# One decoder layer of 512 tokens in f32 on one core: the order of each engine's instructions, up to the second pair of gate's tiles, written in the kernel as lists

## The chip, the cores and the metric

The kernel runs on one core of a Trainium2 chip. The core has five engines with a queue of instructions each: PE (TensorE, matmuls, with a second row PEld for loading weights into the array), DVE (VectorE), ACT (ScalarE), POOL (GpSimd) and SP (SyncE, which here only issues transfers). ACT and POOL issue transfers too. An engine runs its own instructions in the order in which they stand in its queue; between engines, semaphores hold an instruction back until its inputs are made and its output's place is free.

The metric is the device time of one execution in microseconds (us), the median of several runs.

## The reference

One layer of a hybrid decoder: 512 tokens, width 2048, all in float32. The input projection feeds eight forgetting-attention heads (FoX) and eight heads of a sparse attention (NSA) with a compressed, a selected and a windowed branch; their outputs go through one output projection, and a SwiGLU feed-forward of width 5632 follows.

```python
h = _rms_norm(x, attn_norm)
proj = h @ w_in                       # FoX q, k, v, forget gate; NSA q, three k/v pairs, gates
...
s = einsum("bqhd,bkhd->bhqk", qf_b, kf) * scale + cq[..., None] - cum_f[:, :, None, :]
o_fox = einsum("bhqk,bkhd->bqhd", softmax(s, causal), vf)
...
o_nsa = g[0] * o_c + g[1] * o_s + g[2] * o_w
x = x + concat([o_fox, o_nsa]) @ w_out
h = _rms_norm(x, ffn_norm)
x = x + (silu(h @ w_gate) * (h @ w_up)) @ w_down
```

## The kernel before

**Arithmetic.** Every operand of a matmul is held as two parts of the type fp32r, a high part and a low part. ACT makes the high part by a copy that rounds (`split`, lines 87 and 192), DVE then subtracts it from the value to make the low part (lines 84 and 193), and PE adds up three products: high by high, high by low, low by high (`mm` and `mm3t`, line 254). So each operand costs one step on ACT, one on DVE behind it, and PE can't finish with it before both. Large projections are done in a form with seven products of half-size blocks in the place of eight; the sums of blocks that this needs ("forms", made by DVE at lines 991 to 1009 from the input, by `sums` for the weights of gate and up) are operands as well.

**Stages.** In order of time: the first projection with warm-up matmuls ahead of it (0 to 50 us); the projections of NSA's keys and values and their norms (to about 200 us); the heads of NSA and the first of FoX, interleaved with the projections that feed the next ones (to 440 us); the other FoX heads, with projections in the seven-product form (to 640 us); the output projection, `po` (to 795 us); gate and up, `q`, in 22 pairs of column tiles with four weight tiles each (to 1626 us); the down projection, `pd`, to the end.

In attention, a head's scores `s_f` (or `s_s`, `s_w`) go from PE to DVE, which adds the bias `nbf` that POOL made and takes maxima and sums into the statistics `st_f` (line 617); ACT applies the exponential (line 623) and scales (line 632); PE turns the result (`pT_f`, line 648), ACT and DVE split the turned copy into `pt_f`, and PE multiplies it by the values. For the norms of q and k, squares `sq` and `sb` are added, split into `fr_...` (the high part by ACT, the low one by DVE) and summed over the head by a matmul with ones (`ss_...`, line 483).

**What sets the order.** The kernel emits its instructions from Python generators that are advanced by hand, piece by piece. The framework has a planner that then arranges the instructions of each engine by costs and priorities of its own, keeping the dependencies. Two things fix the order in parts: `add_manual_dep` with the class PACE, which ties a transfer behind an instruction of another engine, and `tc.keep_in_program_order`, which is applied through `pin` to whatever `tt` (DVE) and `act` (ACT) emit once `pinned[0]` is set: to "compute" in the output projection (line 1543) and to "all" behind it (line 1580), where `load` (transfers issued by SP) is kept in order as well. Ahead of line 1543 all of the order is the planner's.

**Gate's start.** `fetch` loads a weight tile into a buffer (`r`, `ca` or `cb`), `sums` makes its sums on DVE (three steps of line 84), and `parts` makes the high part on ACT and the low part on DVE. Tile 0 is in `r`, tile 1 in `cb`. A tile then serves 2 x 14 products of its high part and 14 of its low part. Between these stand the last forms of the layer's input: `raw6` and `raw7`, whose parts go into `bigm`, and the residual `x1_15`.

The loop over gate and up:

```python
for j in range(NJ):
    for which in range(2):
        ...
        for g in range(NG):
            i = (2 * j + which) * NG + g
            if 3 <= i < LAST - 1:
                sums(i + 2)
            if 3 <= i < LAST:
                parts(i + 1)
                fetch(i + 4)
            ...
            w = split_w.pop(i)
```

Of the kernel before, what the change touches and what calls it, by code (L numbers as in the profile page):

```python
# [12 lines left out]
OP = mybir.AluOpType  # L13
# [60 lines left out]

@with_exitstack
def hybrid_layer(ctx: ExitStack, tc: tile.TileContext, xT, vec, ffb, wfg, wfirst, win, cmpw, wout, wos, wgu, wdn, out):
    nc = tc.nc
    pinned = [False]

    def pin(ins):  # L80
        return tc.keep_in_program_order(ins) if pinned[0] else ins

    def tt(*args, op):
        return pin(nc.vector.tensor_tensor(*args, op=op))  # L84

    def act(*args, **kw):
        return pin(nc.scalar.activation(*args, **kw))  # L87
# [40 lines left out]
    def sum_weights(after, steps=None):  # L128

        step = next(wsums if steps is None else steps, None)  # L130
        if step is not None:
            d = nc.gpsimd.dma_start(step[0], step[1], **step[2])  # L132
            tc.add_manual_dep(d.ins, after.ins.name, PACE)
# [51 lines left out]
    def split(dst, src, scale=None, neg=None):  # L185

        if scale is None:
            h = act(dst[:, 0], src, AF.Copy)
            tt(dst[:, 1], src, dst[:, 0].bitcast(F32), op=OP.subtract)
            return h  # L190
        else:
            nc.scalar.activation(dst[:, 0], src, AF.Copy, scale=scale)
            nc.vector.scalar_tensor_tensor(dst[:, 1], src, scale, dst[:, 0].bitcast(F32),
                                           op0=OP.mult, op1=OP.subtract)
# [4 lines left out]
    def split2(dst, src, scale=None):  # L199
# [4 lines left out]
        else:  # L204
            h = act(dst[0], src, AF.Copy, scale=scale)
            nc.vector.scalar_tensor_tensor(dst[1], src, scale, dst[0].bitcast(F32), op0=OP.mult, op1=OP.subtract)
# [46 lines left out]
    def mm(o, w, x, j=1, **kw):  # L253
        nc.tensor.matmul(_like(o, j), w, _in_turn(x, j), **kw)  # L254
# [6 lines left out]
    def mm3(o, lh, ll, rh, rl, start, stop):  # L261
        nc.tensor.matmul(o, lh, rh, start=start, stop=False)
        nc.tensor.matmul(o, lh, rl, start=False, stop=False)  # L263
        nc.tensor.matmul(o, ll, rh, start=False, stop=stop)
# [46 lines left out]
    nc.scalar.dma_start(vt, vec)  # L311
# [7 lines left out]
    nc.vector.memset(onesf, 1.0)  # L319
    ones = pers.tile([P, P], FR, name="ones")  # L320
    nc.vector.tensor_copy(ones, onesf)

    def rsqrt(dst, src, n, tmp, whole=True):

        nc.scalar.activation(dst, src, AF.Ln, scale=1.0 / n, bias=EPS)
        nc.scalar.activation(dst, dst, AF.Exp, scale=-0.5)
        nc.scalar.activation(tmp, dst, AF.Square)
        nc.vector.scalar_tensor_tensor(tmp, src, n * EPS, tmp, op0=OP.add, op1=OP.mult)  # L328
        if whole:
            nc.vector.tensor_scalar(tmp, tmp, -0.5 / n, 1.5, op0=OP.mult, op1=OP.add)  # L330
            nc.vector.tensor_tensor(dst, dst, tmp, op=OP.mult)
        else:
            nc.vector.scalar_tensor_tensor(dst, tmp, -3.0 * n, dst, op0=OP.add, op1=OP.mult)

    def colsum(o, src, fr):

        split2(fr, src)
        nc.tensor.matmul(o, ones, fr[0], start=True, stop=False)
        nc.tensor.matmul(o, ones, fr[1], start=False, stop=True)
# [16 lines left out]
    nc.gpsimd.iota(E, pattern=[[-1, T]], base=384, channel_multiplier=1, allow_small_or_imprecise_dtypes=True)  # L356
    nc.gpsimd.affine_select(E, E, pattern=[[-1, T]], compare_op=OP.is_ge, fill=FAR, base=384, channel_multiplier=1)

    dc = xn.tile([P, NB, 32], F32, name="dc")
    nc.gpsimd.iota(dc, pattern=[[P, NB], [-16, 32]], base=-31, channel_multiplier=1, allow_small_or_imprecise_dtypes=True)  # L360
    mc = xn.tile([P, NB, 32], F32, name="mc")
    nc.vector.tensor_scalar(mc, dc, 0.0, None, op0=OP.is_ge)
    nc.gpsimd.affine_select(dc, dc, pattern=[[P, NB], [-16, 32]], compare_op=OP.is_ge, fill=FAR, base=-31, channel_multiplier=1)

    trif = ftile("trif")
    nc.gpsimd.memset(trif, 1.0)
    nc.gpsimd.affine_select(trif, trif, pattern=[[1, T]], compare_op=OP.is_ge, fill=0.0, base=0, channel_multiplier=-1)

    gains = ap_.tile([P, 6], F32, name="gains")
    nc.vector.tensor_scalar_mul(gains, vt[:, 0:6], -0.5 / HD)  # L370
    nc.vector.tensor_scalar_mul(gains[:, V_NQ:V_NQ + 1], gains[:, V_NQ:V_NQ + 1], -SCALE)
    nc.vector.tensor_scalar_mul(gains[:, V_FQ:V_FQ + 1], vt[:, V_FQ:V_FQ + 1], -SCALE)
# [6 lines left out]
    nc.vector.tensor_tensor(rowsf, ident[:, :64], ident[:, 64:], op=OP.add)  # L379
    rows = xn.tile([P, 64], FR, name="rows")  # L380
    nc.vector.tensor_tensor(rows, rowsf, rowsf[:, 31:32].to_broadcast([P, 64]), op=OP.add)

    rows3 = xn.tile([P, 2, 3, 32], FR, name="rows3")
    for n in range(3):
        nc.vector.tensor_copy(rows3[:, :, n], rows.bitcast(F32).rearrange("p (g c) -> p g c", g=2))
# [7 lines left out]
    def scaled(z, name, early=False):  # L393
        t = oxp.tile([P, T], F32, tag="ox", name=f"t_{name}", bufs=OXB) if early else ftile(f"t_{name}")
        if early:
# [3 lines left out]
            nc.vector.tensor_tensor(t.rearrange("p (l b n) -> p b n l", l=16, b=2), b, c, op=OP.mult)  # L399
        else:  # L400
            nc.vector.tensor_tensor(_apart(t), _mixed(z), _apart(rstd), op=OP.mult)
# [17 lines left out]
    def squares(name, z, laid=_apart):  # L419
# [3 lines left out]
        nc.scalar.activation(_apart(sq[half]), laid(z[half]), AF.Square)  # L423
        nc.scalar.activation(_apart(sb[half]), laid(z[second_half]), AF.Square)
        nc.vector.tensor_tensor(sq[half], sq[half], sb[half], op=OP.add)
        return sq

    def square_sums(name, sq, tag, bufs=1):
# [6 lines left out]
        for i in range(NB):  # L435
            nc.tensor.matmul(o[:, i], fr[:, i * P:(i + 1) * P], ones[:, :2], start=(i == 0), stop=(i == NB - 1), skip_group_check=True)
        return o

    def factors(name, o):
# [4 lines left out]
        nc.vector.tensor_tensor(v, o[:, :, 0], eps_col, op=OP.add)  # L444
        nc.scalar.activation(y, v, AF.Ln, scale=1.0 / n)
        nc.scalar.activation(y, y, AF.Exp, scale=-0.5)
        nc.scalar.activation(w, y, AF.Square)
        nc.vector.tensor_tensor(w, v, w, op=OP.mult)
        nc.vector.tensor_scalar(w, w, -0.5 / n, 1.5, op0=OP.mult, op1=OP.add)
        nc.vector.tensor_tensor(qs, w, y, op=OP.mult)  # L450
        nc.vector.scalar_tensor_tensor(iqs, v, 1.0 / n, qs, op0=OP.mult, op1=OP.mult)
# [18 lines left out]
    def normed(name, gain, tag, bufs=5):  # L470
# [5 lines left out]
        nc.scalar.activation(sq[half], t[half], AF.Square)  # L476
        nc.vector.tensor_tensor(sb[half], t[second_half], t[second_half], op=OP.mult)
        nc.vector.tensor_tensor(sq[half], sq[half], sb[half], op=OP.add)
# [4 lines left out]
        nc.tensor.matmul(o, ones, fr, start=True, stop=True)  # L483
# [3 lines left out]
        nc.vector.scalar_tensor_tensor(t, t, gain, y, op0=OP.mult, op1=OP.mult)  # L487
# [4 lines left out]
        else:  # L492
            r = ap_.tile([P, KV], FR, tag=tag, name=name, bufs=bufs)
            if name[:2] == "ks":
                with_compressed[name] = r[:, :64 + T]
                if name == "ks1":
                    nc.scalar.activation(r[:, :64], Kc1.bitcast(F32), AF.Copy)
# [7 lines left out]
    def values(pair, gcols=None):  # L505
# [10 lines left out]
        for c in range(4):  # L516
# [6 lines left out]
            else:  # L523
# [6 lines left out]
                for hi, ks in his:  # L530
                    nc.scalar.activation(hi[:, :, :256], st[:, ks], AF.Copy)
                    nc.scalar.activation(hi[:, :, 256:288], g[:, ks], AF.Copy)
                hi = [hi[:, n] for hi, ks in his for n in range(ks.stop - ks.start)]
                lo = []
                for n in range(2):
                    t = loose(f"wl_{name}{n}").rearrange("p (k c) -> p k c", k=2)
                    lo += [t[:, kk] for kk in range(2)]
                    if n == 0:
                        nc.vector.tensor_tensor(t, st[:, :2], his[0][0][:, :2, :256].bitcast(F32), op=OP.subtract)
                    else:  # L540
                        for kk in range(2):
                            nc.vector.tensor_tensor(t[:, kk], st[:, 2 + kk], hi[2 + kk][:, :256].bitcast(F32), op=OP.subtract)
                for x, ks in his:
                    nc.vector.tensor_tensor(x[:, :, 288:320], g[:, ks], x[:, :, 256:288].bitcast(F32), op=OP.subtract)
                wp = [[x[:, :320] for x in hi], lo, [x[:, :288] for x in hi]]
                cols = [320, 256, 288]
            for b in range(2):
                for some in turns_of(range(4), 3):
                    for p, kk, xp in some:
                        x = xg[4 * c + kk]  # L550
                        n = 2 * xp or p
                        for t in range(2):
                            at = slice((2 * b + t) * P, (2 * b + t + 1) * P)
                            (nc.tensor.matmul if gcols is not None else mm)(  # L554
# [1583 lines left out]
```

## Time and profile before

| what | value |
|---|---|
| median of 3 runs | 2031.21 us (2030.35 to 2033.46) |
| the profiled execution's own time | 2031.23 us |
| its span, from the first instruction to the last | 2029.5 us |
| instructions in the profile | 36414 |
| mean clock granted to PE | 0.999 of full speed |
| transfers | 432.39 MB, mean 213 GB/s |

Times within the profile count from the start of the span. "Busy" is the time in which an engine has an instruction under way; a matmul is counted from its start to its end although the next one starts well before that, so a short pause in the row of starts need not show as idle time. "Idle before, releaser" is the time for which an engine had nothing under way ahead of an instruction, and the instruction elsewhere whose end let it go on. In a timeline, a row gives the start, the busy time, the engine, the line, the operation, the tiles (without their numbers) and the shapes; xN joins N instructions that follow each other closely. In the rows by stretches the columns are the stretch, its length, the busy times, the clock granted to PE (1.00 is full speed), the share of the transfer engines and GB/s.

### The profile page before, as it was taken

The page shows a single profiled execution, that of the slowest core. Times are in us where ns is not written, and L with a number is a line of the kernel's source. Part 1 is how long each engine was busy: PE and PEld are TensorE (multiplying, and loading weights), DVE is VectorE, ACT ScalarE, POOL GpSimd, SP SyncE. Part 2 cuts the span into 40 slices and gives each one's busy share as a digit, 9 for nine tenths or more (in the row PEclk, how much of TensorE's full clock was granted, in tenths as well). Part 3 has the DMA queues.
Part 4 walks back from the last instruction along what each step waited for, and adds up shares of the span by engine and source line. Part 5 has one row for each costly group of instructions (what it writes and reads, how often), then busy time and mean ns, then how long its engine had stood idle before and what let it go on. Part 6 is the DMA issues. An engine that isn't in the chain of part 4 may idle for free.

```text
span 2029.5 us, 36414 instructions
## 1 busy us (share of the span) xinstructions
PE 2002.8 (99%) x14341; PEld 1884.8 (93%) x14341; DVE 1781.6 (88%) x2725; ACT 1080.9 (53%) x1430; POOL 321.0 (16%) x481
## 2 busy tenths in 40 slices
PE   9999999999999999999999999999999999999999
PEld 8878988899998998999999999999999988888887
DVE  6678779888787977999999999999999998888897
ACT  6565555567676555434444443444344455666564
POOL 1032332422221011111111111111111000001000
PEclk9999999999999999999999999999999999999999
DMA  5686786967775675676777878878777798579974
GB/s 210 215 185 171 178 191 174 219 179 212 234 203 177 211 245 169 173 214 200 219 207 211 218 206 201 229 197 200 221 186 203 208 356 300 155 232 315 354 201 143
DMA packets 154062, 432.39 MB, mean 213 GB/s; under 512 B 18777, under 2 KB 26969, under 8 KB 153890
## 3 DMA queue, kind: packets, MB, share of 16 engines
q1 hardware_dynamic: 102176, 297.60, 44.0%
q0 software_dynamic: 44560, 106.19, 25.7%
q10 hardware_dynamic: 7154, 26.27, 3.4%
q8 instruction: 112, 1.84, 0.4%
q14 instruction: 60, 0.49, 0.1%
HBM read 393.54 MB, written 128.73 MB: 257 GB/s over the span
## 4 chain that ended last, share of the span: by engine, by line
PE 79%; DVE 8%; issue 7%; ACT 3%; DMA 2%; POOL 1%; ACTq 0%; POOLq 0%; DVEq 0%
PE q L254 41%; PE pd L254 20%; PE po L254 4%; PE ps_qn L254 2%; PE ps_vf L254 2%; PE ps_kf L254 1%; PE ps_vs L254 1%; PE ps_vs L554 1%; PE ps_kw L254 1%; PE ps_first L254 1%; PE ps_qf L254 1%; DMA x1r<-x1d 1%; POOL osum L132 1%; DVE wq_o L84 0%; PE on L263 0%
## 5 line engine op out<-in xcount | busy, mean ns | idle before, releaser
L87 ACT ACTIVATE bigm<-r 128x1792 fp32r<-128x1792 f32 x174 | 298.1, 1713 | 432.2 <-PE q L254 299.2
L84 DVE TENSOR_TENSOR bigm<-r,bigm 128x1792 fp32r<-128x1792 f32 x174 | 351.3, 2019 | 3.7 <-ACT bigm L87 3.1
L84 DVE TENSOR_TENSOR r<-r 128x512 f32<-128x512 f32 x522 | 266.5, 510 | 17.3 <-DMA r<-wgu 5.2
L132 POOL DMA_DIRECT2D wsum<-wdn x176 | 120.0, 688 | 691.8 <-ACT bigm L87 603.0
L254 PE MATMUL q<-formx,bigm 128*128 128x256 f32 x1848 | 215.3, 276 | 2.2 <-ACT bigm L87 2.2
L254 PE MATMUL q<-forma,bigm 128*128 128x256 f32 x1848 | 214.1, 275 | 0.3 <-ACT bigm L87 0.3
L254 PE MATMUL q<-bigm 128*128 128x256 f32 x1848 | 213.8, 275 | 0.0
L254 PE MATMUL q<-formy,bigm 128*128 128x256 f32 x1848 | 213.8, 275 | 0.0
L254 PEld LDWEIGHTS q<-formx,bigm 128*128 128x128 f32 x1848 | 211.5, 193 | 2.4 <-ACT bigm L87 2.4
L254 PEld LDWEIGHTS q<-forma,bigm 128*128 128x128 f32 x1848 | 210.1, 192 | 1.0 <-ACT bigm L87 0.7
L254 PEld LDWEIGHTS q<-bigm 128*128 128x128 f32 x1848 | 210.0, 192 | 0.2 <-DVE bigm L84 0.2
L254 PEld LDWEIGHTS q<-formy,bigm 128*128 128x128 f32 x1848 | 210.0, 192 | 0.2 <-DVE tmp_r L328 0.2
L254 PE MATMUL pd<-bigm 128*128 128x512 f32 x900 | 202.4, 379 | 0.0
L254 PEld LDWEIGHTS pd<-bigm 128*128 128x128 f32 x900 | 170.1, 189 | 24.1
L84 DVE TENSOR_TENSOR bigm<-wd,bigm 128x1024 fp32r<-128x1024 f32 (+1 forms) x62 | 107.7, 1737 | 22.0 <-ACT bigm L87 21.7
L87 ACT ACTIVATE bigm<-wd 128x1024 fp32r<-128x1024 f32 (+1 forms) x62 | 90.9, 1465 | 33.5 <-DMA wd<-wsum 28.1
L254 PE MATMUL pd<-bigm,formx 128*128 128x512 f32 x444 | 99.3, 379 | 0.0
L87 ACT ACTIVATE bigm<-rawm 128x768 fp32r<-128x768 f32 (+2 forms) x72 | 65.7, 922 | 62.8 <-PE pd L254 38.0
L254 PEld LDWEIGHTS pd<-bigm,formx 128*128 128x128 f32 x444 | 83.9, 189 | 11.9
L254 PE MATMUL po<-bigm,wp_o 128*128 128x512 f32 (+1 forms) x464 | 92.5, 349 | 1.5 <-ACT wp_o L87 0.9
L84 DVE TENSOR_TENSOR bigm<-rawm,bigm 128x768 fp32r<-128x768 f32 (+2 forms) x72 | 75.5, 1058 | 15.8 <-ACT bigm L87 15.4
L254 PEld LDWEIGHTS po<-bigm,wp_o 128*128 128x128 f32 x464 | 76.7, 190 | 10.6 <-ACT wp_o L87 1.5
(584 smaller groups left out, 3816.1 us busy)
## 6 DMA issues: line engine op xcount, KB each, us to landing
r<-wgu SPq DMA_DIRECT2D x174, 512.0 KB, 4.1
wsum<-wdn POOLq DMA_DIRECT2D x176, 256.0 KB, 4.9
rawm<-ad SPq DMA_DIRECT2D x44, 512.0 KB, 7.3
wd<-wdn SPq DMA_DIRECT2D x40, 512.0 KB, 6.0
wd<-wsum SPq DMA_DIRECT2D x40, 512.0 KB, 7.0
ad<-cb ACTq DMA_DIRECT2D x22, 896.0 KB, 5.6
fsump<-win POOLq DMA_DIRECT2D x72, 256.0 KB, 5.1
rawm<-ad SPq DMA_DIRECT2D x44, 384.0 KB, 3.6
```

The source lines that it names most:

```text
L84: return pin(nc.vector.tensor_tensor(*args, op=op))
L87: return pin(nc.scalar.activation(*args, **kw))
L132: d = nc.gpsimd.dma_start(step[0], step[1], **step[2])
L254: nc.tensor.matmul(_like(o, j), w, _in_turn(x, j), **kw)
L554: (nc.tensor.matmul if gcols is not None else mm)(z[2 * b + t][:, :cols[n]], x[:, xp, at], wp[n][kk], start=(c == 0 and kk == 0 and n == 0 ...
```

## The change

All calls on the engines go through wrappers named `pe`, `dve`, `sca`, `pool` and `sp`, which record each instruction as it is emitted. At one point of the gate loop, with the first weight tile of the second pair (`j == 1`, `which == 0`, `g == 0`), `close_order` takes what each engine has recorded so far and ties each instruction behind the one that the engine's list names before it. The lists are five strings of indices in the order of emission, a run "at+n" standing for at to at+n: 5428 instructions for PE, 1265 for DVE, 875 for ACT, 293 for POOL, 243 for SP. The ties have the class NoSync: they set the order within an engine and carry no semaphore. A further string, FIRST, could tie the engines' sequences to each other; it is empty. The first instruction that an engine emits behind that point is tied behind the last of its list. `pin` does nothing while the lists are open, and keeps the order of emission afterwards whatever `pinned[0]` says. No instruction, shape, buffer or dependency on data is changed.

```diff
+SCHED = mybir.DependencyInfo(mybir.DependencyClass.NoSync, mybir.DependencyReason.SCHED_ONLY)
+
+FIRST = """
+
+"""
+
+ORDERS = ("""
+0+250 252+33 251 286+127 416+3 414+1 420+50 473+2 478+4 471+1 476+1 483 486+1 484+1 488+34 524+7 523 532+14
...
+4128+2 4126+1 4131+1224 5358+10 5356+1 5369+58
+""", """
+0+1 6+4 2+2 91 11+1 99 5 13 15 14 17 20 18 16 19 22 21 23 26 29 24 32 25 28 27 35 38 41 30 44 31 34 33 47 50 37
...
+1183+2 1188 1187 1190+2 1189 1194+1 1193 1197 1196 1199+2 1198 1205 1202+2 1207+3 1206 1211 1215+2 1227 1212+2
+1219+3 1218 1226 1223+2 1236 1228+1 1231 1230 1232+2 1239 1235 1242 1240+1 1237+1 1249 1254 1246 1251+2 1250
+1243 1255 1257 1260 1258+1 1261+2 1244 1264 1247 1245 1248 1256
+""", """
...
+""")
+
+
+class Ordered:
+
+    def __init__(self, tc, engine):
+        self.tc, self.engine, self.done, self.last, self.open = tc, engine, [], None, True
+
+    def __getattr__(self, name):
+        f = getattr(self.engine, name)
+
+        def call(*args, **kw):
+            r = f(*args, **kw)
+            if self.open:
+                self.done.append(r.ins)
+            elif self.last is not None:
+                self.tc.add_manual_dep(r.ins, self.last, SCHED)
+                self.last = None
+            return r
+
+        return call
+
+    def close(self, written):
+
+        self.open = False
+        order = []
+        for run in written.split():
+            at, n = map(int, (run + "+0").split("+")[:2])
+            order += range(at, at + n + 1)
+        assert not order or sorted(order) == list(range(len(self.done))), (len(order), len(self.done))
+        order = [self.done[i] for i in order]
+        for a, b in zip(order, order[1:]):
+            self.tc.add_manual_dep(b, a.name, SCHED)
+        if order:
+            self.last = order[-1].name
+        return order
+
+
+def close_order(tc, engines):
+
+    orders = [iter(e.close(written)) for e, written in zip(engines, ORDERS)]
+    before = None
+    for letter, n in re.findall(r"([A-Z])(\d*)", FIRST):
...
     nc = tc.nc
+    engines = pe, dve, sca, pool, sp = [Ordered(tc, e) for e in (nc.tensor, nc.vector, nc.scalar, nc.gpsimd, nc.sync)]
     pinned = [False]
 
     def pin(ins):
-        return tc.keep_in_program_order(ins) if pinned[0] else ins
+        return ins if dve.open else tc.keep_in_program_order(ins)
 
     def tt(*args, op):
-        return pin(nc.vector.tensor_tensor(*args, op=op))
+        return pin(dve.tensor_tensor(*args, op=op))
...
     def load(dst, src):
-        d = nc.sync.dma_start(dst, src)
+        d = sp.dma_start(dst, src)
         return tc.keep_in_program_order(d) if pinned[0] == "all" else d
...
                 w = split_w.pop(i)
+                if j == 1 and which == 0 and g == 0:
+                    close_order(tc, engines)
```

The other edits of the diff write `pe`, `dve`, `sca`, `pool` or `sp` for `nc.tensor`, `nc.vector`, `nc.scalar`, `nc.gpsimd` or `nc.sync`, and rename two local variables `pool` to `place_`.

More of the change, by code (lines that the diff above doesn't have):

```diff
@@ L1 @@
 import itertools
+import re
 from contextlib import ExitStack
@@ L72 @@
 OTHERS = ((4, 3, 2, 1), (5, 5, 0, 1), (6, 1, 1, 0), (3, 4, 1, 1))
+SCHED = mybir.DependencyInfo(mybir.DependencyClass.NoSync, mybir.DependencyReason.SCHED_ONLY)
+FIRST = """
+"""
+ORDERS = ("""
[92 rows of a table added]
+""")
[30 more added lines that the diff above has]
+    for letter, n in re.findall(r"([A-Z])(\d*)", FIRST):
+        for _ in range(int(n or 1)):
+            ins = next(orders["PVAGS".index(letter)])
+        if before is not None:
+            tc.add_manual_dep(ins, before, SCHED)
+        before = ins.name
 @with_exitstack
@@ L378, in hybrid_layer @@
     rowsf = ftile("rowsf")[:, :64]
-    nc.vector.tensor_tensor(rowsf, ident[:, :64], ident[:, 64:], op=OP.add)
+    dve.tensor_tensor(rowsf, ident[:, :64], ident[:, 64:], op=OP.add)
     rows = xn.tile([P, 64], FR, name="rows")
-    nc.vector.tensor_tensor(rows, rowsf, rowsf[:, 31:32].to_broadcast([P, 64]), op=OP.add)
+    dve.tensor_tensor(rows, rowsf, rowsf[:, 31:32].to_broadcast([P, 64]), op=OP.add)
     rows3 = xn.tile([P, 2, 3, 32], FR, name="rows3")
     for n in range(3):
-        nc.vector.tensor_copy(rows3[:, :, n], rows.bitcast(F32).rearrange("p (g c) -> p g c", g=2))
+        dve.tensor_copy(rows3[:, :, n], rows.bitcast(F32).rearrange("p (g c) -> p g c", g=2))
     rcol = ap_.tile([P, NB], F32, name="rcol")
@@ L435, in square_sums @@
         for i in range(NB):
-            nc.tensor.matmul(o[:, i], fr[:, i * P:(i + 1) * P], ones[:, :2], start=(i == 0), stop=(i == NB - 1), skip_group_check=True)
+            pe.matmul(o[:, i], fr[:, i * P:(i + 1) * P], ones[:, :2], start=(i == 0), stop=(i == NB - 1), skip_group_check=True)
         return o
@@ L475, in normed @@
         sb = ap_.tile([P, T], F32, tag="sb", name=f"sb_{name}")
[L476 to L478 removed]
+        sca.activation(sq[half], t[half], AF.Square)
+        dve.tensor_tensor(sb[half], t[second_half], t[second_half], op=OP.mult)
+        dve.tensor_tensor(sq[half], sq[half], sb[half], op=OP.add)
         yield POST
@@ L482, in normed @@
         split2([fr[half], fr[second_half]], sq[half])
-        nc.tensor.matmul(o, ones, fr, start=True, stop=True)
+        pe.matmul(o, ones, fr, start=True, stop=True)
         yield
@@ L486, in normed @@
         rsqrt(y, o, float(HD), ftile(f"tmp_{name}"), False)
-        nc.vector.scalar_tensor_tensor(t, t, gain, y, op0=OP.mult, op1=OP.mult)
+        dve.scalar_tensor_tensor(t, t, gain, y, op0=OP.mult, op1=OP.mult)
         if tag == "q":
@@ L553, in values @@
                             at = slice((2 * b + t) * P, (2 * b + t + 1) * P)
-                            (nc.tensor.matmul if gcols is not None else mm)(
+                            (pe.matmul if gcols is not None else mm)(
                                 z[2 * b + t][:, :cols[n]], x[:, xp, at], wp[n][kk],
@@ L890, in hybrid_layer @@
     for _ in range(WARM):
-        nc.tensor.matmul(warm[:, :P], onesf, onesf, start=True, stop=True)
+        pe.matmul(warm[:, :P], onesf, onesf, start=True, stop=True)
     first = [ps.tile([P, T], F32, tag=tag, name=f"ps_first{i}", bufs=n)
@@ L990, in summed @@
         d = ftile(name).rearrange("p (f t) -> p f t", f=2)
-        nc.vector.tensor_tensor(d, a, b, op=op)
-        nc.vector.tensor_tensor(d[:, 0], d[:, 0], d[:, 1], op=OP.add)
+        dve.tensor_tensor(d, a, b, op=op)
+        dve.tensor_tensor(d[:, 0], d[:, 0], d[:, 1], op=OP.add)
         return d
@@ L1115, in pair @@
         ok = ps.tile([P, T], F32, tag="t", name=f"ss_{k}", bufs=2)
-        nc.tensor.matmul(ok, ones, fr, start=True, stop=True)
+        pe.matmul(ok, ones, fr, start=True, stop=True)
         oq = square_sums(q, sq, "t", 2)
@@ L1272, in add_squares @@
             if n == 0:
-                pin(nc.vector.tensor_copy(acc, sq))
+                pin(dve.tensor_copy(acc, sq))
             else:
```

342 lines of the change are left out of this document (171 added, 171 removed), and 84 rows, old and new, of the table ORDERS.

## The prediction

> **What bounds the kernel now.** I read the page's busy times first, then the busy time of TensorE (PE) in stretches cut where the work changes, then what PE waited for, and last the timelines around the longest waits.
>
> ```profile
> span 2029.5 us, 36414 instructions
> PE 2002.8 (99%) x14341; PEld 1884.8 (93%) x14341; DVE 1781.6 (88%) x2725; ACT 1080.9 (53%) x1430; POOL 321.0 (16%) x481
> 0.00:50.00 50.00, 48.42 (x215) 1.00 0.58 209
> 50.00:200.00 150.00, 146.93 (x828) 1.00 0.68 191
> 200.00:440.00 240.00, 234.08 (x1548) 1.00 0.78 187
> 440.00:640.00 200.00, 192.13 (x1562) 1.00 0.74 218
> 640.00:700.00 60.00, 59.36 (x386) 1.00 0.48 157
> 700.00:790.00 90.00, 89.01 (x547) 1.00 0.68 224
> 790.00:850.00 60.00, 57.44 (x469) 0.97 0.58 166
> 850.00:2029.00 1179.00, 1175.43 (x8801) 1.00 0.76 225
> 816.88 809.69 PE q L254 x7242
> ```
>
> In the rows of stretches, the columns are the stretch, its length, PE's busy time with its matmuls, the granted clock, and DMA. PE is idle for 2029.5 − 2002.8 = 26.7 us in all. The last row is one piece of the chain that ended last: from 816.88 on, 7242 matmuls of gate and up run for 809.69 us with nothing between them. The order lists end in that piece (the second pair of gate's tiles), so **only what stands ahead of 816.88 can change**, and an earlier arrival there is carried to the end one for one: behind it PE is the bound, and weight loads go out as buffers come free, hence with it. The idle time ahead: 1.58, 3.07, 5.92, 7.87, 0.64, 0.99 and 2.56 us, together 22.6.
>
> ```profile
> PE s_f L262 <- DVE st_f L617: 2.8, 3, 1.1
> PE q L254 <- ACT bigm L87: 2.5, 2, 2.2
> PE pT_f L648 <- ACT p_f L632: 2.3, 4, 1.0
> PE ss_ks L483 <- DVE fr_ks L84: 2.0, 1, 2.0
> PE ss_kf L483 <- DVE fr_kf L84: 1.9, 1, 1.9
> PE ps_vf L254 <- ACT sb_qf L424: 0.8, 1, 0.8
> PE s_s L600 <- DVE st_s L617: 0.8, 1, 0.8
> ```
>
> These are PE's waits (total us, times, longest). None is a stage that lacks an engine: they are some thirty single matmuls, nearly all of attention, that come up before VectorE (DVE) or ScalarE (ACT) has made one small operand. Over the whole view the waits are 2.6 us (3 times) in 50 to 200, 5.7 (8) in 200 to 440, and 7.4 (12) in 440 to 640.
>
> A wait costs more than the idle time shown, since PE's pipeline drains. In the chain row, matmuls of 256 columns start 809.69 / 7242 = 0.112 us apart, while one lasts 0.276 us:
>
> ```profile
> L254 PE MATMUL q<-formx,bigm 128*128 128x256 f32 x1848 | 215.3, 276 | 2.2 <-ACT bigm L87 2.2
> ```
>
> So each wait adds about 0.16 us. With that, what could be had is 3.1 us, 7.0 us and 9.4 us in the three stretches, **19.5 us**.
>
> **The change, part by part.** It adds and removes no instruction and no buffer. The lists hold PE's 5428, DVE's 1265, ACT's 875, POOL's 293 and SP's 243 instructions; the string that would order engines against each other is empty, and the links within an engine carry no semaphore. PE's list differs from the old order in some 350 places, by at most 47 positions; POOL's and SP's in a handful, so that transfers keep their order; DVE's in 1016 of 1265 and ACT's in 550 of 875. It is a re-queueing of DVE and ACT.
>
> *Attention, 50 to 640.* The longest wait here that stands in the middle of matmuls:
>
> ```profile
> 393.93 0.81 PE L254 MATMUL ps_qf<-bigm,wp_qf 128*128 128x512 f32 x3
> 396.60 0.47 PE L483 MATMUL ss_kf<-fr_kf,ones 128*128 128x512 f32 x1 [1.86 <-DVE fr_kf L84]
> 392.94 1.21 DVE L84 TENSOR_TENSOR wq_qf<-ws_qf,wp_qf 128x1024 fp32r<-128x1024 f32 x1
> 394.41 0.73 DVE L617 CUSTOM_DVE_ANT_0 p_f<-s_f,nbf,qs_qf 128x512 f32<-128x512 f32 x1
> 395.52 0.94 DVE L84 TENSOR_TENSOR fr_kf<-sq_kf,fr_kf 64x512 fp32r<-64x512 f32 x1
> ```
>
> ss_kf waits for fr_kf, DVE's last step of k's squares. DVE had no gap ahead of it: it was making forms (d, f, acc at L991 to L1009) that later products use. In the list fr_kf stands ten places earlier: adding up the durations of what leaves and what enters its front, 5.5 us of DVE work less is ahead of it, against 1.86 us of lateness. The same sum for fr_ks (66.6 us) is 1.4 us against 2.0; for the statistics st_s and st_w and the turned copies pt_s, pt_w between 278 and 363 it is 2.7 to 8.6 us, against 0.2 to 0.8 each. In 440 to 640 the cover is thinner: st_f 1.9 to 4.2 us, against 0.6 to 1.1; p_f at 482.1 is only 1.8 us earlier on ACT, by one scaling ahead of its three fellows (L632), against 1.0; one st_f (624.4) hangs on POOL's bias nbf too, whose place is 1.8 us earlier. In a dozen places the lists also put 0.2 to 1.1 us of other matmuls in front of the waiting one.
>
> Nothing disappears: the forms are made later. Their cover is PE's work until their own use, and DVE's free time, 240 − 196.28 and 200 − 169.79 us:
>
> ```profile
> 200.00:440.00 240.00, 234.08 (x1548) 213.25 (x1547) 196.28 (x501) 139.67 (x318) 80.39 (x117) 1.00 0.78 187
> 440.00:640.00 200.00, 192.13 (x1562) 184.15 (x1561) 169.79 (x323) 150.98 (x275) 48.15 (x76) 1.00 0.74 218
> ```
>
> (DVE is the third busy time in these rows, ACT the fourth.) With 82% and 85% of DVE filled, some forms and low parts become the next thing late; and operands chained PE to ACT to DVE to PE can't be re-queued beyond their input. I take 2.4 of 3.1, 6 of 7.0 and 7 of 9.4 us: **−15.4 us**. The ends are nothing (all handed back) and the full 19.5.
>
> *Start.* DVE's list puts four small steps (rowsf, rows, rows3, mc) and the gains ahead of the cast of w0p that PE's first real matmul waits for:
>
> ```profile
> 4.64 0.43 DVE L905 CAST w0p<-w 128x512 fp32r<-128x512 f32 x1 [2.95 <-DMA w<-wfirst]
> 5.22 2.04 PE L254 MATMUL ps_first<-bigm,w0p 128*128 128x512 f32 x4
> ```
>
> DVE is free for 2.95 us there, which hides most; a few short ones need the loaded vector. Between 0 and 1 us; I take **+0.3**.
>
> *Output projection, 640 to 700.* DVE's list has the sums ft and osums_a ahead of low parts of the output weights (wq_o) that PE and the next weight load need; DVE had gaps there. Adding durations, the last of those low parts comes some 3.5 us later with 2.4 us of slack, 1.1 us, and the 0.64 us of idle time may go. Between −0.6 and +2.4: **+0.5**. 700 to 790: **0**.
>
> *Gate's start* speaks most against the change:
>
> ```profile
> 791.86 1.61 DVE L84 TENSOR_TENSOR r<-r 128x512 f32<-128x512 f32 x3 [0.59 <-DMA r<-wgu]
> 793.39 2.02 DVE L84 TENSOR_TENSOR bigm<-raw,bigm 128x1792 fp32r<-128x1792 f32 x1
> 795.33 2.02 DVE L84 TENSOR_TENSOR bigm<-r,bigm 128x1792 fp32r<-128x1792 f32 x1
> 799.00 1.61 DVE L84 TENSOR_TENSOR cb<-cb 128x512 f32<-128x512 f32 x3 [1.65 <-DMA cb<-wgu]
> 800.52 0.68 DVE L84 TENSOR_TENSOR x<-po,xr 128x512 f32<-128x512 f32 x1
> 791.39 1.70 ACT L87 ACTIVATE bigm<-raw 128x1792 fp32r<-128x1792 f32 x1 [1.75 <-DVE raw L84]
> 793.56 1.70 ACT L87 ACTIVATE bigm<-r 128x1792 fp32r<-128x1792 f32 x1 [0.47 <-DVE r L84]
> 795.31 4.96 PE L254 MATMUL q<-forma,bigm 128*128 128x256 f32 x42 [0.34 <-ACT bigm L87]
> 802.44 3.79 PE L254 MATMUL q<-formx,bigm 128*128 128x256 f32 x17 [2.17 <-ACT bigm L87]
> 799.00:803.00 4.00, 1.83 (x15) 0.94 0.94 311
> 803.00:807.00 4.00, 4.00 (x25) 0.63 0.59 197
> ```
>
> Weight tile 0 (r) is summed, its high part made (ACT, 1.70), then its low part (DVE, 2.02), and 42 products run; tile 1 (cb) follows. The list puts raw6's low part (the 2.02 at 793.39, which must wait for ACT) ahead of r's sums, and cb's sums, which wait for a transfer, ahead of r's low part. ACT ends raw6's high part at 793.1; low part and r's sums are then done at 796.7, r's high part at 798.4, so the products start 3.1 us later than 795.31. Its low part stands behind cb's sums and x: 799.00 + 1.61 + 0.61 + 2.02 = 803.2, and the last 14 products need it: 803.2 + 14 × 0.112 = 804.8, where before cb's products began at 802.44. That is **+2.3 us**; DVE then runs without a gap, so I see no way to win it back.
>
> The clock matters here: in the last two rows it falls after the wait of 2.17 us, and 17 products take 3.79 us, twice their 1.90. [...] After the change the idle stretch is 794.96 to 798.4: the slow products that follow (28 of them by 803.3) still end about when r's low part is ready, so that it costs nothing more there, and cb's wait is gone. If both lots run slow, it is 1.9 us more. Between 0 and 4.2.
>
> **Sum**, against the profiled execution's own time, 2031.23 us (the median of the runs, 2031.21, is the same): −15.4 + 0.3 + 0.5 + 2.3 = −12.3, **2018.9 us**.
>
> **The rivals.**
>
> *A, all queue-bound waits go.* The releasers were ready and only queued, by margins above their lateness in most places. Then 19.5 us, and perhaps 2 of the 4.2 us of idle time elsewhere, less 0.5 to 2.3 us: some −20, 2011 us. Against: DVE's filling, and p_f's and nbf's margins.
>
> *B, the waits move.* What is put off (forms, low parts of projections' weights) turns up late in its own place, and two thirds of the 15.4 us come back: −5.1 + 3.1 = −2, 2029 us. For: 82 to 85% of DVE. Against: ACT and PE hardly idle on the same pieces, and the forms have tens of us until use.
>
> *C, slower: an engine waits at the head of its list while ready work stands behind it.* Lists keep each engine to one sequence whatever lands first. The place is gate's start and wherever DVE's list names an operand that is a transfer or an ACT step away. The price per place is that of cb: 2.3 to 4.2 us. It decides from four or five such places in the 640 us of attention (5 × 3.5 = 17.5 us, over the gain): +5, 2036 us. For: DVE's 1016 shifted places. Against: the lists shift an operand by 3 to 9 us at the most, of the order of DVE's present lateness. [...]
>
> *D, the change doesn't do what it says.* The links add no semaphore, so if the order came out as before, the time is 2031. The listed positions differ, which leaves it little.
>
> **How the numbers follow.** A difference of 0.2%, 4 us, is about what can be told from no change. Chances: forecast (−7 to −17) 0.46; A (beyond −17) 0.18; B and D (−7 to +4) 0.24, of which half is under −4; C 0.12. Faster 0.46 + 0.18 + 0.13 = 0.77; same 0.11; slower 0.12. The range goes from 2007 (A with all the idle time ahead) to 2031 (B and D); above lies most of C.
>
> **What would show it.** Right: PE's idle time in 50 to 640 falls from 16.9 to some 4 us, ss_ks and ss_kf wait no more, and DVE's forms (L991 to L1009) stand later; the first q product comes some 12 us earlier on the clock of the span, but its second lot starts about 9.8 us after the last product of the output projection, not 7.5. Wrong: waits for forms or for wq tiles of about the old sum (B); DVE idle behind an ACT or DMA releaser with PE waiting (C); no shift at all (D). If gate's second tile waits no longer than before, the 2.3 us was mis-read.

## The result, and the profile after

The changed kernel takes 2020.82 us (median of 4 runs, 2018.89 to 2021.34) against 2031.28 (2030.35 to 2033.46): a ratio of 0.9945 with a 95% interval of 0.9928 to 0.9962. That is 10.5 us less. The profiled execution is the fastest of the four, 2018.89 us, so its 12.3 us are the upper end of what the change brings.

From the page after, the span and the busy times:

```profile
span 2017.2 us, 36451 instructions
PE 1994.9 (99%) x14341; PEld 1885.5 (93%) x14341; DVE 1794.1 (89%) x2725; ACT 1082.4 (54%) x1430; POOL 327.6 (16%) x481
```

From the rows by stretches after (the stretch, its length, PE busy, the clock, DMA):

```profile
0.00:50.00 50.00, 48.72 (x223) 1.00 0.61 220
50.00:200.00 150.00, 149.70 (x854) 1.00 0.71 196
200.00:440.00 240.00, 235.59 (x1606) 1.00 0.78 191
440.00:640.00 200.00, 193.68 (x1535) 1.00 0.72 212
640.00:700.00 60.00, 60.00 (x451) 1.00 0.64 207
700.00:790.00 90.00, 85.57 (x483) 0.98 0.63 201
790.00:850.00 60.00, 58.63 (x518) 1.00 0.65 173
```

From PE's waits after (every instruction now has line 187, where the wrapper calls the engine; total us, times, longest):

```profile
PE q L187 <- ACT bigm L187: 3.6, 2, 2.5
PE s_f L187 <- DVE st_f L187: 3.4, 5, 0.9
PE q L187 <- DVE bigm L187: 2.2, 2, 2.0
PE ps_vf L187 <- DVE f L187: 2.0, 1, 2.0
PE pT_f L187 <- ACT p_f L187: 1.4, 2, 0.7
PE ps_vf L187 <- ACT wp_vf L187: 1.3, 1, 1.3
PE ss_ks L187 <- DVE fr_ks L187: 0.3, 1, 0.3
```

And the end of gate and up in the chain after, which ended at 816.88 + 809.69 = 1626.57 before:

```profile
904.15 710.08 PE q L187 x6356
```

It ends at 1614.23, 12.34 us earlier. The reader is to see three things. The wait of ss_ks, 2.0 us before, is down to 0.3, and in 50 to 200 almost nothing is idle (0.3 us; 3.07 before). Two large waits are new, ps_vf for f and for wp_vf. And q, the first products of gate, waits longer than before, 5.8 us in place of 2.5.

Since PE's instructions are the same in both, each matmul's start after can be subtracted from the same matmul's start before. I call the difference **PE's lead** (the median of 13 neighbours, so that swapped places don't matter). It says where time was gained, in us, by the clock of the profile before:

| at | 8 | 50 | 200 | 401 | 410 | 440 | 640 | 700 | 784 | 820 | end |
|---|---|---|---|---|---|---|---|---|---|---|---|
| after | 0.90 | 1.74 | 6.51 | 14.90 | 12.21 | 11.99 | 13.07 | 14.45 | 15.87 | 12.46 | 12.34 |
| gained since | | 0.84 | 4.77 | 8.39 | -2.69 | -0.22 | 1.08 | 1.38 | 1.42 | -3.41 | -0.12 |

So 16 us are gained up to gate's start, with a loss of 2.7 us at 401 to 410 inside, and 3.4 us are lost at gate's start. In 440 to 640, where the prediction had its largest term, there is 1.1 us.

**The loss at 401 to 410.** In the timeline after, ACT, POOL and PE (start, busy time, in brackets the idle time before and what ended it):

```profile
386.12 0.40 ACT L187 ACTIVATE f<-d 128x256 fp32r<-128x256 f32 x1
390.22 0.33 ACTq L187 DMA_DIRECT2D ckb<-cumd  x1
390.65 1.06 ACT L187 ACTIVATE wp_vf<-ws_vf 128x1024 fp32r<-128x1024 f32 x1 [4.13 <-POOL nbf L187]
388.87 0.83 POOL L187 DMA_DIRECT2D osum<-osum  x1 [3.55 <-DMA osum<-wos]
389.46 0.73 POOL L187 TENSOR_SCALAR nbf<-ckb,ncq,qs_qf 128x128 f32<-128x128 f32 x1
391.76 1.60 PE L187 MATMUL ps_vf<-wp_vf,bigm 128*128 128x256 f32 x12 [1.26 <-ACT wp_vf L187]
395.36 1.83 PE L187 MATMUL ps_vf<-wp_vf,bigm 128*128 128x256 f32 x14 [2.00 <-DVE f L187]
```

ACT's list names a transfer, ckb, ahead of wp_vf. The transfer overwrites a buffer that POOL's nbf still reads, and POOL itself stood 3.55 us behind another transfer. ACT was idle for 4.13 us at the head of its list, and then PE waited twice for what stood behind. In the kernel before, the same two instructions of ACT:

```profile
400.84 0.33 ACTq L857 DMA_DIRECT2D ckb<-cumd  x1
401.26 1.06 ACT L87 ACTIVATE wp_vf<-ws_vf 128x1024 fp32r<-128x1024 f32 x1 [0.27 <-issue]
```

So the list didn't move ckb: it stood there before as well, ahead of the same four instructions, and ACT waited 0.27 us. What is new is when ACT comes to it. ACT is done with what stands ahead 14.5 us sooner (386.5 in place of 401.0), but the last nbf that reads the buffer starts only 10.9 us sooner (389.46 in place of 400.36).

**The loss at gate's start.** PE, DVE and ACT in the timeline after:

```profile
781.47 3.39 PE L187 MATMUL q<-forma,bigm 128*128 128x256 f32 x28 [2.48 <-ACT bigm L187]
786.82 3.16 PE L187 MATMUL q<-forma,bigm 128*128 128x256 f32 x14 [1.95 <-DVE bigm L187]
789.77 5.20 PE L187 MATMUL q<-formx,bigm 128*128 128x256 f32 x42
778.04 1.60 DVE L187 TENSOR_TENSOR r<-r 128x512 f32<-128x512 f32 x3
779.72 1.70 ACT L187 ACTIVATE bigm<-r 128x1792 fp32r<-128x1792 f32 x1 [3.66 <-DVE r L187]
782.62 1.61 DVE L187 TENSOR_TENSOR cb<-cb 128x512 f32<-128x512 f32 x3 [2.98 <-DMA cb<-wgu]
784.75 2.02 DVE L187 TENSOR_TENSOR bigm<-r,bigm 128x1792 fp32r<-128x1792 f32 x1
```

The first 28 products start 2.48 us late, the 14 of the low part wait 1.95 more. DVE stood idle for 2.98 us in front of cb's sums while r's low part, 2.02 us of work that was ready once ACT had made the high part at 781.4, stood behind them.

### The profile page after: what moved, and what is told of

It is laid out like the page before. It is cut to its first block, busy times and chain, and to the rows that moved or that the text cites. A ratio compares the mean times of both kernels' runs of the same rounds, so it can differ in the third digit from the quotient of the medians.

```text
span 2017.2 us, 36451 instructions
## 1 busy us (share of the span) xinstructions
PE 1994.9 (99%) x14341; PEld 1885.5 (93%) x14341; DVE 1794.1 (89%) x2725; ACT 1082.4 (54%) x1430; POOL 327.6 (16%) x481
## 4 chain that ended last, share of the span: by engine, by line
PE 85%; issue 5%; DVE 4%; ACT 2%; POOL 2%; DMA 2%; SPq 0%; ACTq 0%; POOLq 0%; DVEq 0%
PE q L187 38%; PE pd L187 20%; PE po L187 8%; PE ps_qn L187 4%; PE ps_vf L187 2%; PE ps_vs L187 2%; PE ps_first L187 2%; PE on L187 2%; DVE bigm L187 1%; PE ps_kf L187 1%; POOL nbf L187 1%; PE ps_kw L187 1%; PE ps_ks L187 1%; PE s_s L187 1%; PE s_w L187 1%
## 5 line engine op out<-in xcount | busy, mean ns | idle before, releaser
L187 DVE TENSOR_TENSOR bigm<-rawm,bigm 128x768 fp32r<-128x768 f32 (+2 forms) x72 | 75.5, 1058 | 16.8 <-ACT bigm L187 16.5
```

The lines of the kernel that those rows point to most:

```text
L187: r = f(*args, **kw)
```

## The experiments

All are the changed kernel with other lists. "Lead" is PE's lead of the profiled execution over the kernel before, at the same points as above.

| kernel | median us | ratio (95%) | 401 | 410 | 440 | 640 | 784 | 820 | end |
|---|---|---|---|---|---|---|---|---|---|
| after | 2020.82 | 0.9945 (0.9928 to 0.9962) | 14.9 | 12.2 | 12.0 | 13.1 | 15.9 | 12.5 | 12.3 |
| after_again | 2020.13 | 0.9947 (0.9930 to 0.9964) | 14.8 | 10.4 | 10.2 | 11.6 | 14.2 | 9.7 | 10.2 |
| lists_before | 2030.32 | 0.9999 (0.9990 to 1.0009) | 0.2 | 0.2 | 0.2 | 0.2 | 1.2 | 1.4 | 1.7 |
| pe_only | 2031.18 | 1.0003 (0.9994 to 1.0012) | -2.5 | -1.6 | -1.8 | -2.2 | -1.0 | -0.7 | -0.5 |
| gate_only | 2034.93 | 1.0023 (1.0014 to 1.0032) | -0.8 | -0.8 | -0.8 | -0.9 | -0.8 | -5.2 | -4.4 |
| gate_before | 2015.48 | 0.9928 (0.9913 to 0.9943) | 15.2 | 12.7 | 12.5 | 13.7 | 16.5 | 16.0 | 16.2 |
| ckb_late | 2015.90 | 0.9929 (0.9914 to 0.9944) | 14.4 | 15.0 | 14.7 | 16.1 | 18.9 | 15.5 | 15.4 |
| att_before | 2022.80 | 0.9960 (0.9946 to 0.9974) | 14.5 | 10.8 | 10.4 | 10.3 | 13.1 | 8.8 | 7.9 |
| qs_early | 2019.35 | 0.9944 (0.9929 to 0.9959) | 15.1 | 12.7 | 12.5 | 15.6 | 17.9 | 14.5 | 14.7 |
| pool_pairs | 2018.88 | 0.9940 (0.9925 to 0.9955) | 14.5 | 12.3 | 12.1 | 14.6 | 17.4 | 14.0 | 14.6 |
| wq_apart | 2019.04 | 0.9946 (0.9930 to 0.9963) | 14.7 | 12.4 | 12.2 | 14.0 | 16.1 | 12.9 | 12.2 |
| combo | 2011.17 | 0.9902 (0.9885 to 0.9918) | 14.4 | 15.4 | 15.2 | 18.4 | 20.9 | 20.1 | 20.3 |
| combo2 | 2010.05 | 0.9899 (0.9885 to 0.9914) | 15.1 | 16.2 | 16.0 | 19.7 | 22.3 | 21.8 | 20.9 |

### Is it the order alone, and whose?

**lists_before**: all five lists spell the order of the kernel before.

```diff
-ORDERS = (the change's lists)
+ORDERS = (the emission numbers in the order in which the kernel before runs them)
```

> The changed kernel with all five lists spelling the order of the kernel before. My theory: the ties cost nothing and only the order counts, so that the time is that of the kernel before, 2031.2 within 1.5 us, and PE's lead stays within 0.5 us of zero all along. The rival: a part of the gain comes from the way of tying (no semaphores between neighbours, transfers no longer pinned); then 2025 to 2029.

2030.32 us, ratio 0.9999, a lead of 0.2 us up to 640. Within the interval, which is 2 us to either side, the way of tying costs and brings nothing: the gain is the order's. (1 us of lead between 700 and 784 comes with the old order too: PE's waits for wp_o, 1.2 us in the kernel before, are 0.4 us here. Why is open.)

**pe_only**: the change's list for PE, the old order for the others.

```diff
 PE:                  the change's list
-DVE, ACT, POOL, SP:  the change's lists
+DVE, ACT, POOL, SP:  the order before
```

> The change's list for PE alone; DVE's, ACT's, POOL's and SP's lists spell the old order. My theory: the gain is a re-queueing of DVE and ACT, and PE's 350 shifted places bring under 2 us by 784 us: 2029 to 2031. The rival: PE's list does half of it, by putting ready products ahead of the one that waits: 5 us or more, 2026 or less.

2031.18 us, with a lead between 0.2 and -2.5 from 50 us on: PE's own list by itself brings nothing. DVE's list alone, with the old order on the other engines, gives no time, though 10 to 13 us of the lead at 395 us were expected of it: the new and the old order wait on each other. ACT's list alone, or all lists but one, was not run. So that DVE and ACT make the gain is shown by what is left over, not directly, and whether they need PE's list beside theirs is open.

### Gate's start

**gate_before** has the change's lists up to 785 us and the old order behind; **gate_only** the reverse.

```diff
 every list:  the elements that ran ahead of 785 us before, in the change's order
-             the rest in the change's order
+             the rest in the order before          (gate_only: the two orders swapped)
```

> The lists of the change up to 785 us, and behind that (on the clock of the profile before) every engine's list spells the old order, so that gate's first tile is summed and split ahead of raw6's low part and of cb's sums. My theory: the order of DVE at gate's start costs 3.5 us of the change (PE's lead over the kernel before falls from 16.0 us at 784 to 12.4 us at 820). Then the lead stays at about 15 to 16 us, the first tile's high part starts about 0.3 us behind the last product of the output projection and not 2.5, and the time is 2017.3 us (2020.8 less 3.5). The rival: PE arrives 16 us earlier and the weight tiles' transfers are late for it whatever DVE does; then the lead falls to 12.4 all the same and the time stays at 2020.8.

> The old order on all engines up to 785 us, and the change's lists from there to the second pair of gate's tiles. My theory: the order at gate's start costs by itself, whatever PE's lead: PE falls 3.5 us behind the kernel before between 784 and 820, and the time is 2034.5. The rival: it costs only where PE arrives 16 us early; then the time is 2031.

gate_before: 2015.48 us, 5.3 less than after; the lead falls by 0.5 us between 784 and 820, not by 3.4. gate_only: 2034.93 us, slower than the kernel before (1.0023, all of the interval above 1), with a fall of 4.4 us. The order there costs by itself, whatever PE's lead, and the rival falls. In the timeline of gate_before, PE and DVE:

```profile
778.21 4.85 PE L181 MATMUL q<-forma,bigm 128*128 128x256 f32 x42
786.48 5.69 PE L181 MATMUL q<-formx,bigm 128*128 128x256 f32 x34 [3.42 <-ACT bigm L181]
783.03 1.61 DVE L181 TENSOR_TENSOR cb<-cb 128x512 f32<-128x512 f32 x3 [4.07 <-DMA cb<-wgu]
```

The first tile's 42 products run through without a wait. PE then waits 3.42 us for the second, more than before (2.17): DVE idles until cb's transfer has landed at 783.0, and ACT and PE follow. That wait is left, and no order run here wins it back: with the change's order the second tile doesn't wait only because the first one ends later.

### ACT's wait for POOL

**ckb_late**: one number of ACT's list is moved.

```diff
 ACT:
-449 484 465 452 448 453 429 454
+449 465 452 448 453 429 484 454
```

> The lists of the change with one instruction moved: ACT's issue of the transfer into ckb (head 1) stands behind the forms' and wp_vf's high parts (at about 394 us) in place of ahead of wp_vf. My theory: ACT stood 4.1 us at the head of its list for POOL to be done with the buffer, while wp_vf, kf and f, which were ready, stood behind it; without that PE's two waits (1.26 us for wp_vf at 391.8, 2.00 us for f at 395.4) go, PE's lead at 400 is 15 us and not 12.2, and the time is 2017.5. The rival: wp_vf's raw weights or DVE's next step are late as well, and the lead grows by less than 1 us: 2020.

2015.90 us, 4.9 less than after, and the lead goes from 14.4 to 15.0 over the place where it fell by 2.7. By the profiled executions it is 3.0 us; after's other executions can lose more here (after_again, below). ACT and PE in its timeline:

```profile
386.66 1.04 ACT L184 ACTIVATE wp_vf<-ws_vf 128x1024 fp32r<-128x1024 f32 x1
389.86 0.41 ACT L184 ACTIVATE f<-acc 128x256 fp32r<-128x256 f32 x1
390.99 0.33 ACTq L184 DMA_DIRECT2D ckb<-cumd  x1
392.62 2.05 PE L184 MATMUL ps_vf<-wp_vf,bigm 128*128 128x256 f32 x16 [0.23 <-ACT sb_qf L184]
```

wp_vf starts at 386.66, 4 us sooner, and PE's two waits, 3.26 us, are one of 0.23. This place is the rival C of the prediction, on ACT: one instruction that waits for a buffer, at the head of a fixed list, with ready work behind it. The lists kept it there; they didn't put it there.

### Why 440 to 640 brought only 1 us

**att_before**: the old order in this stretch.

```diff
 every list:  the elements between 441 and 640.5 us
-             in the change's order
+             in the order before
```

> The lists of the change, except that the stretch from 441 to 640.5 us (on the clock of the profile before) is spelled in the old order on all five engines. My theory: the lists gain nothing there, because what PE waits for hangs on POOL's bias nbf, which stands in the same place behind the same small steps qs_qf; then PE's lead is 12 to 13 us at 640 with either order and the time is 2020.8, at most 1.5 us more. The rival, which is my prediction's term: the lists gain 7 us there by taking DVE's and ACT's queue out of the way, and lose as much by an inversion of their own; then the old order, which has only its old waits (7.4 us idle), gives the same lead too, but the waits differ: with the old order the waits for fr_kf, pt_f and t_vf come back in place of those for st_f. A third reading, that the lists do gain 7 us and PE's lead was lost elsewhere, gives 2028.

2022.80 us. From 410 to 640 the lead falls by 0.5 us with the old order and grows by 0.9 with the new (1.1 in a second execution): the lists are worth some 1.5 us there. My theory is too simple, though: with the old order the waits for t_vf, pt_f and wq_kf are back (0.7, 0.4 and 0.4 us). The lists did remove those, but other waits came in their place. The waits of s_f for st_f are 2.8 us (3 times) in the old order and 3.4 (5 times) in the new, and 2.4 us are new: for fr_kf (0.8, twice), t_kf and po's bigm (0.7 each) and ps_kf's bigm (0.2). On the same pieces PE waits 12 times before, 7.4 us in all, and 12 times after, 7.2 us. The share of st_f is the largest, and only that was followed up. What makes st_f late? After, POOL, DVE and PE for head 3:

```profile
484.92 2.50 POOL L187 TENSOR_SCALAR nbf<-ckb,ncq,qs_qf 128x512 f32<-128x512 f32 x2 [3.77 <-issue]
485.00 1.22 DVE L187 TENSOR_TENSOR wq_kf<-ws_pair,wp_kf 128x1024 fp32r<-128x1024 f32 x1
487.70 0.75 DVE L187 CUSTOM_DVE_ANT_0 p_f<-s_f,nbf,qs_qf 128x512 f32<-128x512 f32 x1 [1.49 <-POOL nbf L187]
488.52 0.61 PE L187 MATMUL s_f<-kf,qq 128*128 128x256 f32 x3 [0.62 <-DVE st_f L187]
```

(POOL's row joins the steps of two tiles, 512 and 384 columns wide.) p_f waits for POOL's bias, which starts when the last small step of qs_qf on DVE is done (at 484.75). In relation to the end of the head's first scores on PE, the masked bias is ready 2.2 us late on the mean of heads 2 to 7 before, and 3.3 us after. Three experiments cut this chain at three links.

**qs_early** moves the eight small steps of qs_qf forward in the heads 1 to 7 (here head 3, DVE):

```diff
-831 826 827 828 830 832 838 829 833 834 835 836 837
+831 832 826 827 833 834 835 836 828 830 838 829 837
```

> The lists of the change; for the FoX heads 1 to 7 the eight small steps of qs_qf (five on DVE at 0.16 us, three on ACT at 0.2 us) are moved forward to where their inputs are ready, 2 to 5 us earlier. My theory: POOL's nbf starts when qs_qf is done, and the first scores' p_f on DVE waits for nbf, so that s_f waits for st_f; with qs_qf early, nbf starts 2 us or more earlier, the five waits for st_f (3.4 us, with the drains some 4.2) go, and the time is 2016.6. The rival: p_f is held by its own place in DVE's list, behind wq_kf's low part, or by POOL's transfers; then the waits shrink to about half and the time is 2018.8 to 2020.

**pool_pairs** makes and masks each tile in turn (POOL's numbers for one pair of tiles; 8 such pairs, and 4 more swaps at later tiles):

```diff
-139 145 140 146
+139 140 145 146
```

> The lists of the change with one thing altered, on POOL: for the first two tiles of each FoX head the order of the four steps of nbf is made, masked, made, masked, in place of made, made, masked, masked. My theory: the first p_f needs only the first tile, so it gets its bias one step (0.66 us) earlier, PE's five waits for st_f shrink from 3.4 us to under 1, and PE's lead at 640 grows from 13.1 to 15.5 us: 2018. The rival: masking takes as long as it saves, since a masking step between two others measured up to 2 us on POOL; then nothing changes, 2020.8.

**wq_apart** moves one wq of DVE behind the first p_f in the heads 2 to 6 (head 3):

```diff
-837 843 839 840
+837 839 843 840
```

> The lists of the change; for the FoX heads 2 to 6 the one low part of a projection's weights (wq, 128x1024, 1.22 us) that DVE makes while POOL makes the first nbf tile stands behind that head's first p_f in place of ahead of it. PE uses that wq 3.9 us or more after p_f's end less 1.1. My theory: POOL's step of 128x512 takes 0.77 us with nothing like that beside it and 1.85 with it, so the five steps fall from 1.85 to 0.77, the first p_f comes 1.08 us earlier, PE's waits for st_f fall from 3.4 to under 1, and PE's lead at 640 grows by 3 us to 16: 2018. The rival: POOL's step is long for another reason (the first of a head, just behind a transfer's issue); then it stays at 1.85, DVE has only lost time, and the time is 2020.8 or more.

In 440 to 640 the lead grows by 3.1 us in qs_early, 2.5 in pool_pairs and 1.8 in wq_apart, against 1.1 after (1.1 to 1.4 in the four executions with the change's lists there). The waits for st_f, 3.4 us after, are gone in qs_early, 0.3 in pool_pairs and 1.6 in wq_apart. So POOL's bias was behind the waits for st_f, and none of the three gives all that these cost; the other new waits, 2.4 us, were left alone. In qs_early the next thing is late: its time is in the range of its rival, though not by the rival's way, since s_f now waits for kf. From PE's waits there:

```profile
PE s_f L184 <- DVE kf L184: 1.3, 4, 0.3
```

In wq_apart, POOL and DVE:

```profile
484.49 1.41 POOL L184 TENSOR_SCALAR nbf<-ckb,ncq,qs_qf 128x512 f32<-128x512 f32 x2 [3.78 <-issue]
486.18 0.75 DVE L184 CUSTOM_DVE_ANT_0 p_f<-s_f,nbf,qs_qf 128x512 f32<-128x512 f32 x1 [1.53 <-POOL nbf L184]
486.85 1.22 DVE L184 TENSOR_TENSOR wq_kf<-ws_pair,wp_kf 128x1024 fp32r<-128x1024 f32 x1
```

The same two steps of POOL take 1.41 us in place of 2.50 with wq out of their way, as expected; but wq now stands ahead of the second p_f. By medians the three are 1.5 to 1.9 us under after, but their ratios (0.9940 to 0.9946) are that of after (0.9945) within the intervals: the time doesn't show a gain, and the verdict rests on the waits and the leads.

### Together

**combo** is ckb_late, qs_early and gate_before in one; **combo2** adds pool_pairs and puts qs_qf behind t_kf in two heads.

```diff
 ORDERS:  ckb behind f (ACT), qs_qf early (DVE, ACT), the order before from 785 us on
+combo2:  nbf made and masked in turn (POOL), qs_qf behind t_kf in the heads 3 and 4 (DVE)
```

> Three edits together: ckb's transfer behind wp_vf on ACT, qs_qf early for the heads 1 to 7, and the old order from 785 us on. My theory: they hit different stages and add up: 2.7 us at 400, 2.0 us in 440 to 640 and 3.5 us at gate's start on top of the change's lead of 12.3 us, 20.5 us in all: a span of 2009 and a time of 2011 to 2012. The rival: what is saved in attention is taken back at gate's start, where the weight tiles' transfers are the next late thing; then not below 2015, the time of the old order at gate's start alone.

> The three edits of combo, POOL's nbf steps in pairs for all heads, and for the heads 3 and 4 the last four steps of qs_qf on DVE behind t_kf in place of ahead of it. My theory: combo's four waits of s_f for kf (1.3 us) come from qs_qf standing ahead of t_kf; two of the four go, and the pairs take 0.66 us from each first p_f: 1 us less than combo, 2010.2. The rival: those are not on PE's path any more, and the time stays at 2011.2.

2011.17 us (2009.73 to 2011.93): the three add up. combo2: 2010.05 (2009.69 to 2010.41), ratio 0.9899 (0.9885 to 0.9914), 20 us under the runs of the kernel before beside it (2030.12) and faster than both. Its expected step was wrong, since s_f still waits for kf four times (1.5 us), so its 1.1 us over combo are not laid to that edit, and the ranges of the two kernels overlap.

### The spread of the runs

**after_again**: the changed kernel once more, unaltered.

> The changed kernel itself, on the chip of this call. The median of its runs was 2020.8, its profiled execution 2018.9. My theory: the 2 us between them lie in the first 8 us (matmuls at half their rate for 1.1 us more or less) and in the weight tiles' transfers at gate's start, so that another profile shows PE's lead at 784 between 15 and 16.1 us and a loss of 3 to 5.5 us at gate's start. The rival: the profiled execution was typical, and the lead and the loss are the same within 0.3 us.

2020.13 us; profiled, 2021.02, where after's profile took 2018.89. Both readings fall: most of the 2 us lies neither in the first 8 us nor at gate's start but at 401 to 410, where the lead falls by 4.4 and not 2.7 us. PE's waits there are the same 1.3 and 2.0 us. What differs is the clock behind them. The stretch behind the two waits, after:

```profile
396.00:400.00 4.00, 4.00 (x38) 1.00 0.95 242
```

and after_again:

```profile
396.00:400.00 4.00, 4.00 (x25) 0.61 0.99 252
```

25 matmuls in place of 38 in the same 4 us. The same lists, the same waits, and in one execution the clock falls. At the start, the lead at 8 us is between 0 and 1.1 us in kernels with the same lists there.

## Why the prediction was right or wrong

The time was forecast at 2018.9 with a range of 2007 to 2031; 2020.8 is inside, and the sign was right. But the sum, -12.3, met the profiled -12.3 by luck: its terms were off in both directions, and the medians differ by 10.5. PE's idle time in 50 to 640 was to fall from 16.9 to some 4 us; by the rows of stretches it fell to 11.0 (0.3, 4.4 and 6.3).

| step | forecast, us | measured, us (the lead with its sign turned) |
|---|---|---|
| start | +0.3 | -1.7 (0.9 of it within 8 us) |
| 50 to 200 | -2.4 | -4.8 |
| 200 to 440 | -6 | -5.5 (8.4 gained, 2.9 lost) |
| 440 to 640 | -7 | -1.1 |
| 640 to 784 | +0.5 | -2.8 |
| gate's start | +2.3 | +3.4 |

**What bounds it** was right: from 1000 us on the lead is 12.34 us to the end. (In the other executions it moves by up to 1.6 us there, in att_before.)

**50 to 200**: the mechanism (releasers that only queued) was right, the size too small. The three waits that I counted gave 2.7 of the 4.8 us. The rest came from places where a start was 0.1 to 0.3 us late and the list of waits shows nothing: ss_kw at 111.61 starts 0.48 us behind the start before it, and 0.22 us in the changed kernel.

**640 to 784**: the forecast was a loss, and it is a gain. The low parts that were to come late hold nothing up; PE waits nowhere between 640 and 779 us after, where it waited 1.6 us before. And 1.0 us of the 2.8 comes with the old order too (lists_before).

**Start**: no loss either; the first real matmul starts at 5.21 us (5.22 before). 0.8 us comes from waits between 20 and 37 us that went; the other 0.9 varies between executions (0.9 in gate_only too, with the old order there).

**440 to 640** is the step that failed: 7 us were forecast and 1.1 came. The cover of "st_f 1.9 to 4.2 us" was queue taken away on DVE and ACT. POOL's bias was named for one place only, though DVE's waits of the kernel before in this stretch are led by it:

```profile
DVE p_f L617 <- POOL nbf L863: 9.1, 11, 1.8
```

In the lists qs_qf ends just about when the first scores end (within 0.2 us in four of the heads 2 to 7), as if the bias cost little; it costs 2.5 us for two tiles. On the mean of these heads qs_qf is 0.5 us later than before, later in three and earlier in three; the rest of the 1.1 us by which the bias is later lies on POOL, whose step of 128x512 takes 1.8 us on the mean of these heads in place of 1.0. Rival B ("the waits move") holds here, with the place qs_qf and nbf, not forms: 12 waits before, 12 after. What the other new waits (fr_kf, t_kf, bigm) hang on stays open.

**Gate's start**: the mechanism held to the step, raw6 ahead of r, cb and x ahead of r's low part. The second tile's products were to start 9.8 us behind the last product of the output projection; they start 10.8 behind it (789.77 less 778.99; 7.5 before). The 1 us more is the clock, where I had the slow products hidden in the first wait: the clock was still 1.00 in 781 to 785, behind the first wait, and fell only after the second (0.57 in 787 to 791), and the 14 products of the low part took 2.95 us up to the second tile's (786.82 to 789.77), not the 14 x 0.112 = 1.57 that I had; they had started 0.4 us sooner than forecast. In after's rows by stretches:

```profile
784.00:788.00 4.00, 2.05 (x14) 0.88 0.28 97
788.00:792.00 4.00, 4.00 (x27) 0.69 0.91 294
```

**Rival C** was priced at 2.3 to 4.2 us per place and given four or five places to turn the sign. There were two, gate's start and ckb, of 3.4 and 2.7 us (ckb 4.4 in the second execution): about right in price. The ckb place is not one that the lists made. **A** did not come; combo2 shows that 20 us were to be had, by other lists than the change's. **D** fell with lists_before.

## What to carry to other kernels

A fixed order of an engine's instructions is only as good as the durations behind its deadlines: look for the step that is late by its own engine's price (here POOL's bias, 1.8 us for a step of 128x512, and the 0.16 us steps that feed it), and for instructions at the head of a list that wait for a transfer or a buffer while ready work stands behind them (here ckb, with ACT idle for 4.13 us, and cb, with DVE idle for 2.98). Such an instruction need not have moved: it is enough that its engine comes to it sooner than the one it waits for gets done. Compare the start of each matmul before and after, stage by stage: a sum that comes out right can hide a gain given back.

## What the runs showed of the hardware

**POOL's nbf and DVE's wq get in each other's way.** The same step of POOL (nbf, 128x512) takes 0.76 or 0.77 us at its shortest. In the heads 2 to 6 of the changed kernel it takes 1.83 to 1.86 us, and in each a subtraction of DVE on 128x1024 (wq, 1.22 us) lies beside it. With wq moved apart head 3's two steps fall from 2.50 to 1.41 us. In two heads of the kernel before, POOL's step began 0.22 us ahead of wq: it took 0.76 and 0.77 us, and wq took 1.62. So in each of these seven places one of the two is long; what decides which can't be told from the starts alone, since in three of those heads of the changed kernel POOL's step starts 0.08 to 0.14 us ahead of wq and is the long one all the same.

**The clock can fall after two waits of 2 us and less, and doesn't always.** Two waits of 1.3 and 2.0 us within 6 us slowed the next matmuls (25 in 4 us in place of 38, at a granted clock of 0.61 in place of 1.00) in one execution of a kernel and not in another. At the same place, with waits of 0.8 and 2.0 us, the clock was 0.57 in att_before, and with 1.0 and 2.0 us 1.00 in gate_before: what decides it was not shown.
